# A pair's scale factors taken apart from its rotation, and accumulating DMAs issued some products later, in a two-layer encoder on one Trainium2 core

## The chip, the core and the metric

The kernel runs on one core of a Trainium2 chip. A core has five engines, each with a queue of its own that it works through in order: TensorE (PE, products of a stationary and a moving operand into PSUM banks), VectorE (DVE), ScalarE (ACT), GpSimd (POOL) and SyncE (SP, which here only issues loads). DMAs are issued by an engine's queue (here SP, ACT and POOL) and moved by 16 DMA engines beside it. Engines wait for one another by semaphores: an instruction whose input isn't ready holds up everything behind it on its own engine, and nothing else.

The metric is the device time of one execution in microseconds, the median over several.

## The reference

The reference is an encoder of two layers over 512 tokens of width 1024, all in float32. Layer 0 mixes tokens by gated linear attention, layer 1 by softmax attention, and a gated MLP with a width-3 convolution follows each. The change lies wholly in layer 1's attention:

```python
def attn_mixer(h, w_qkv, q_norm, k_norm, w_out, cos, sin):
    proj = h @ w_qkv
    q, k, v = jnp.split(proj, [...])          # 8 query heads, 2 key/value heads of 128
    q = apply_rope(rmsnorm(q, q_norm), cos, sin)
    k = apply_rope(rmsnorm(k, k_norm), cos, sin)
    ...
    s = jnp.einsum('bkgqd,bksd->bkgqs', q_blk, k) * scale   # four query heads share a kv head
    p = jax.nn.softmax(s, axis=-1)
    ... jnp.einsum('bkgqs,bksd->bkgqd', p, v) ...
    return o @ w_out

def apply_rope(x, cos, sin):
    half = x.shape[-1] // 2
    x1, x2 = x[..., :half], x[..., half:]
    return jnp.concatenate([x1 * cos - x2 * sin, x1 * sin + x2 * cos], axis=-1)
```

The root mean square in `rmsnorm` is one number per token and head, so it commutes with the rotation: a head may be rotated first and scaled afterwards.

## The kernel before, in words

**Split products.** The large products take their operands in the type float32r. Every operand is kept as two parts, `hi` (the value as it is written into that type) and `lo` (the rest), and a product is three matmuls: hi·hi, hi·lo and lo·hi (`mm3`). A product of 128 rows by 512 columns over one chunk of 128 is called a step below; a projection of one tile has 8 chunks (`KC`), that is 8 steps or 24 matmuls.

**Weights.** `Weights` takes weight blocks in a written order. `half(src, n)` gives out the half block that is asked for, and makes one more ahead of need: SP loads a raw block of 1 MB (two buffers `raw`), ACT writes `wh`, and `lo` arises in one of two ways. In `split` DVE subtracts. For the sources in `by_dma` (all the weights of layer 1's attention: `qk_order`, `w_av`, `w_aout`) ACT writes the negated `hi` into `wl`, and POOL issues a DMA that adds `raw` into `wl` (line 125). There are three buffers of `wh` and three of `wl`.

**Attention.** Heads are made in pairs: `kpair` makes the two key heads, `qpair(i)` the query heads 2i and 2i+1, and both go through the generator `roped`, which yields at the end of each small piece of work, so that the caller can weave pieces of several generators into one another. In `roped`, 16 pieces are the steps of the two halves A and B of the pair (their banks of tag `acc`, three in all). Then ACT squares A and B and DVE adds the squares (`qa`). Then come four pieces with one product each of A or B with the norm's weight and a table of cosines or sines (`rt`, DVE, line 627). Then `scale_tok` makes the factors per token and head: PE sums the squares over the partitions (`hs`, line 603), DVE scales and adds epsilon (`hs`, line 607; `hr`, line 186), POOL raises to the power -1/2 (`hr`, line 190), and DVE multiplies the result into `qsc` (line 610). Then four subtractions and additions of 64 rows make the rotated heads (`ry`, lines 636 and 637; on POOL but for the key pair's and query pair 0's subtractions), and at last ACT and DVE split each head into `hi` and `lo` (`q`, lines 643 and 644).

The scores run over 32 blocks, 8 heads by 4 groups of 128 queries, one after the other, with block t as a beat: `scores` (PE `s`, then DVE's maximum `mx` and factor `nb`, then ACT's exponential `p` with the row sum), then the pieces of other generators that `plan[t]` holds, then `turn` of the block four beats earlier (PE transposes `pt`, ACT `pth`, DVE `ptl`), then `shares` (DVE `rc` and the normalised `p`), then every second beat `mix` of a block six beats earlier (PE `po`, and per head a split `oT`). Two banks serve `s`, two `pt`, one `po`. `Q_STEPS` and `Q_READY` say at which beats how many pieces of the query pairs 1 to 3 run: the 16 steps from the first, the rest from the second. Head 2i's first scores stand at beat 8i and need its `hi` and `lo`. `O_STEPS` are the beats at which a step of the output projection (`op`, `out_steps`, line 297) runs; its remaining steps follow after the last beat.

**What sets the order.** The program's order is a wish: the framework's scheduler puts each engine's instructions into a fixed order when the kernel is built, by priority and by when it thinks that inputs are ready, and that order can be read before the kernel runs.

Of the kernel before, what the change touches and what calls it, by code (L numbers as in the profile page):

```python
# [8 lines left out]
F32 = mybir.dt.float32  # L9
# [37 lines left out]
def hybrid_encoder_kernel(  # L47
# [55 lines left out]
    class Weights:  # L103
# [1 line left out]


        def __init__(self):
            self.todo, self.made, self.raw, self.by_dma = [], {}, {}, []

        def add(self, src):  # L110
            for i in range(src.shape[0]):
# [2 lines left out]
        def make(self, key):  # L114
            src, i, h = key
            if h == 0 and (id(src), i) not in self.raw:
                t = sp.tile([P, 4 * S], F32, tag="raw", bufs=2, name=nm("raw"))
                sync.dma_start(t, src[i])
                self.raw[id(src), i] = t
            r = self.raw[id(src), i][:, h * 2 * S : (h + 1) * 2 * S]  # L120
            hi, lo = pair("wh", 3, F32R, "wh"), pair("wl", 3, F32R, "wl")
            if any(src is a for a in self.by_dma):
                act.activation(hi, r, AF.Copy)
                act.activation(lo, r, AF.Copy, scale=-1.0)  # L124
                pool.dma_start(lo.bitcast(F32), r, accum_op=ALU.add)  # L125
# [56 lines left out]
    def rsqrt_eps(src, w, n, scale=None, tag="tiny"):  # L182

        t = tiny(w, n, tag)
        if scale is None:
            dve.tensor_scalar(t, src, EPS, None, ALU.add)
        else:
            dve.tensor_scalar(t, src, scale, EPS, ALU.mult, ALU.add)
        r = tiny(w, n, tag)
        pool.tensor_tensor(r, t, halfneg[:, :w], ALU.pow)  # L190
        return r
# [52 lines left out]
    def mm3(ps, wh, wl, mh, ml, start, stop):  # L244

        mm(ps, wh, mh, start=start, stop=False)  # L246
        mm(ps, wh, ml, start=False, stop=False)  # L247
        mm(ps, wl, mh, start=False, stop=stop)  # L248
# [12 lines left out]
    def token_steps(src, i0, hl, ps, width, per_half):  # L261

        for hf in range(KC // per_half):
            wh, wl = W.half(src, i0 + hf)
            for kk in range(per_half):
                k = hf * per_half + kk
                sl = slice(kk * width, (kk + 1) * width)
                for j in range(NT):
                    js = slice(j * P, (j + 1) * P)
                    xh, xl = hl[k][0][:, js], hl[k][1][:, js]  # L270
                    st, sp_ = k == 0, k == KC - 1
                    mm(ps[j][:, :width], xh, wh[:, sl], start=st, stop=False)
# [8 lines left out]
    def out_steps(src, hl, nxt):  # L281


        pss, ws = {}, {}

        def part(ng, ks):
            if ng not in pss:
                pss[ng] = [bank("s" if ng % 2 else "acc", "op") for _ in range(2)]
            for k in ks:
                hf, kk = divmod(k, 4)  # L290
                if (ng, hf) not in ws:
                    ws[ng, hf] = W.half(src, ng * 2 + hf)
                wh, wl = ws[ng, hf]
                for i, (wt, mv) in enumerate(((wh, hl[k][0]), (wh, hl[k][1]), (wl, hl[k][0]))):
                    for n in range(2):
                        sl = slice((kk * 2 + n) * P, (kk * 2 + n + 1) * P)
                        mm(pss[ng][n], wt[:, sl], mv, start=k == 0 and i == 0, stop=k == KC - 1 and i == 2)  # L297
                yield

        def end(ng):  # L300
            for n in range(2):
                c = ng * 2 + n
                dve.tensor_tensor(x[c], x[c], pss[ng][n], ALU.add)
                nxt.chunk(c)

        yield from part(0, range(6))
        yield from part(1, range(6))
        for ng in range(2):
            yield from part(ng, (6, 7))
            end(ng)  # L310
        for ng in (2, 3):
            yield from part(ng, range(KC))
            end(ng)
# [278 lines left out]
    def attention(norm, nxt):  # L592
# [3 lines left out]
        cos, sin = cs[:, :S], cs[:, S:]  # L596
        r2 = cp.tile([P, NT], F32, name="r2")

        def scale_tok(sq, extra, keep):

            ps = bank("pt", "hs")
            for j in range(NT):
                mm(ps[:, 2 * j : 2 * j + 2], sq[:, j * P : (j + 1) * P], bd, start=True, stop=True)
            t = tiny(8, "hs", "tiny2")
            t3 = t.rearrange("p (j e) -> p j e", e=2)
            bc = lambda a: a.rearrange("p (j o) -> p j o", o=1).to_broadcast([P, NT, 2])
            dve.tensor_tensor(t3, ps[:, :8].rearrange("p (j e) -> p j e", e=2), bc(r2), ALU.mult)
            r = rsqrt_eps(t, 8, "hr", tag="tiny2")
            o = cp.tile([P, 8], F32, name=nm(keep))
            dve.scalar_tensor_tensor(o.rearrange("p (j e) -> p j e", e=2), r.rearrange("p (j e) -> p j e", e=2),  # L610
                                     extra, bc(norm.rtok), ALU.mult, ALU.mult)
            return o

        def roped(i, wcol, extra, keep, tag="acc"):
# [8 lines left out]
            yield  # L623
            wa, wb = prm[:, wcol : wcol + 1], prm[:, wcol + 1 : wcol + 2]
            t = [tmp("u", "rt") for _ in range(4)]
            for dst, src, w, tab in ((t[0], pa, wa, cos), (t[2], pa, wa, sin), (t[1], pb, wb, sin), (t[3], pb, wb, cos)):
                dve.scalar_tensor_tensor(dst, src, w, tab, ALU.mult, ALU.mult)
# [65 lines left out]
        run(qg, 5)  # L693
        run(vg2, 3)
        whole(qg)
        whole(vg2)
# [172 lines left out]
```

## Time and profile before

| | us |
|---|---|
| three runs | 1147.37, 1147.58, 1147.93 (median 1147.58) |
| profiled execution, its own time | 1146.72 |
| its span, from the first to the last instruction | 1145.0 |
| PE busy in the span | 1131.7 (99%) |
| DVE, ACT, POOL busy | 683.7, 485.0, 87.5 |
| granted TensorE clock | 1.000 |

The attention of layer 1 takes the span from about 590 to 780 us. The profile's rows give a start and a duration in us (the waits views: total, times, longest), the engine, the line of the source, the operation and its tiles as out<-in. "[x <-E tile L]" behind a row of the timeline is the idle time of its engine before it and what ended it. Matmuls overlap in the pipeline, so a matmul's own duration is longer than the distance of its start to the next start, and the distance is what it costs.

### The profile page before, as it was taken

How to read it: one execution, taken by the hardware profiler on the slowest of the kernel's cores; microseconds unless marked ns; L12 is line 12 of the kernel's file. 1: busy time of each engine (PE TensorE's matmuls, PEld its weight loads, DVE VectorE, ACT ScalarE, POOL GpSimd, SP SyncE). 2: the span in 40 equal slices, each digit the busy share in tenths (PEclk: the TensorE clock that was granted, in tenths of full speed). 3: DMA queues.
4: the chain of work that ended last, by engine and by line, in shares of the span. 5: the costliest groups of instructions: out<-in, count | busy, mean ns of one | idle time of the engine just before them, and what ended most of it. 6: DMA issues, size and time to landing. Idle time of an engine off the chain costs nothing. (4 is left out here: it accounts for less than half of the span.)

```text
span 1145.0 us, 13049 instructions
## 1 busy us (share of the span) xinstructions
PE 1131.7 (99%) x5280; PEld 942.3 (82%) x5280; DVE 683.7 (60%) x992; ACT 485.0 (42%) x695; POOL 87.5 (8%) x77
## 2 busy tenths in 40 slices
PE   9999999999999999999999999999999999999998
PEld 7888888888888888888888877888888888888887
DVE  5677653577777777633326678745777777762221
ACT  5565233444444444422244656554444444441210
POOL 0214110000000000000004423010000000000000
PEclk9999999999999999999999999999999999999999
DMA  6322211232322323323256532253322322323320
GB/s 228 135 86 74 76 72 37 74 103 81 110 82 102 111 76 108 110 74 111 98 147 160 148 74 74 56 111 111 110 98 86 110 80 104 110 76 127 129 92 19
DMA packets 20412, 113.76 MB, mean 99 GB/s; under 512 B 2432, under 2 KB 2816, under 8 KB 8832
## 3 DMA queue, kind: packets, MB, share of 16 engines
q1 hardware_dynamic: 17328, 102.42, 25.8%
q0 software_dynamic: 2880, 10.49, 4.8%
q8 instruction: 41, 0.67, 0.3%
q14 instruction: 19, 0.16, 0.0%
q10 hardware_dynamic: 144, 0.02, 0.0%
HBM read 100.34 MB, written 2.10 MB: 89 GB/s over the span
## 5 line engine op out<-in xcount | busy, mean ns | idle before, releaser
L134 ACT ACTIVATE wh<-raw 128x1024 fp32r<-128x1024 f32 x160 | 168.8, 1056 | 335.6 <-PE up L247 132.4
L135 DVE TENSOR_TENSOR wl<-raw,wh 128x1024 fp32r<-128x1024 f32 x160 | 198.9, 1244 | 150.2 <-ACT wh L134 149.8
L246 PE MATMUL up<-xhl,wh 128*128 128x512 f32 x704 | 274.3, 390 | 0.0
L248 PE MATMUL up<-xhl,wl 128*128 128x512 f32 x704 | 273.9, 389 | 0.0
L247 PE MATMUL up<-xhl,wh 128*128 128x512 f32 x704 | 273.9, 389 | 0.0
L248 PEld LDWEIGHTS up<-xhl,wl 128*128 128x128 f32 x704 | 132.1, 188 | 27.5
L246 PEld LDWEIGHTS up<-xhl,wh 128*128 128x128 f32 x704 | 132.1, 188 | 27.4
L247 PEld LDWEIGHTS up<-xhl,wh 128*128 128x128 f32 x704 | 132.2, 188 | 27.3
L248 PE MATMUL dn<-gu,wl 128*128 128x512 f32 x352 | 136.9, 389 | 0.0
L246 PE MATMUL dn<-gu,wh 128*128 128x512 f32 x352 | 136.9, 389 | 0.0
L247 PE MATMUL dn<-gu,wh 128*128 128x512 f32 x352 | 136.9, 389 | 0.0
L564 DVE TENSOR_TENSOR u<-up,R 128x512 f32<-128x512 f32 x88 | 60.3, 687 | 52.7 <-PE up L248 52.6
L566 ACT ACTIVATE y<-u,cw 128x512 f32<-128x512 f32 x88 | 71.1, 810 | 21.6 <-DVE u L564 21.6
L248 PEld LDWEIGHTS dn<-gu,wl 128*128 128x128 f32 x352 | 66.1, 188 | 13.8
L247 PEld LDWEIGHTS dn<-gu,wh 128*128 128x128 f32 x352 | 66.1, 188 | 13.7
L246 PEld LDWEIGHTS dn<-gu,wh 128*128 128x128 f32 x352 | 66.1, 188 | 13.7
L297 PE MATMUL op<-oT,wh 128*128 128x512 f32 x256 | 70.6, 394 | 0.0
L568 DVE SCALAR_TENSOR_TENSOR y<-u,cw,y 128x511 f32<-128x511 f32 x88 | 65.9, 751 | 2.9
L567 DVE SCALAR_TENSOR_TENSOR y<-u,cw,y 128x511 f32<-128x511 f32 x88 | 65.5, 745 | 0.6 <-ACT y L566 0.6
L570 ACT ACTIVATE y<-y 128x512 f32<-128x512 f32 x44 | 27.9, 634 | 87.8 <-DVE y L568 87.7
L297 PEld LDWEIGHTS op<-oT,wh 128*128 128x128 f32 x256 | 47.1, 188 | 9.6 <-ACT oT L524 0.3
L125 POOL DMA_DIRECT2D wl<-raw x20 | 17.8, 888 | 461.9 <-ACT wl L124 461.9
(190 smaller groups left out, 1553.3 us busy)
## 6 DMA issues: line engine op xcount, KB each, us to landing
raw<-in_w_up_dram SPq DMA_DIRECT2D x44, 1024.0 KB, 4.8
raw<-in_w_down_dram SPq DMA_DIRECT2D x22, 1024.0 KB, 4.8
wl<-raw POOLq DMA_DIRECT2D x20, 512.0 KB, 4.6
raw<-in_w_vg_dram SPq DMA_DIRECT2D x6, 1024.0 KB, 4.8
raw<-in_w_akq_dram SPq DMA_DIRECT2D x5, 1024.0 KB, 5.1
raw<-in_w_kq_dram SPq DMA_DIRECT2D x4, 1024.0 KB, 4.8
raw<-in_w_gout_dram SPq DMA_DIRECT2D x4, 1024.0 KB, 4.8
raw<-in_w_aout_dram SPq DMA_DIRECT2D x4, 1024.0 KB, 4.8
```

The lines of the kernel that those rows point to most:

```text
L125: pool.dma_start(lo.bitcast(F32), r, accum_op=ALU.add)
L134: act.activation(hi[:, sl], r[:, sl], AF.Copy)
L135: dve.tensor_tensor(lo[:, sl], r[:, sl], hi[:, sl].bitcast(F32), ALU.subtract)
L246: mm(ps, wh, mh, start=start, stop=False)
L247: mm(ps, wh, ml, start=False, stop=False)
L248: mm(ps, wl, mh, start=False, stop=stop)
L297: mm(pss[ng][n], wt[:, sl], mv, start=k == 0 and i == 0, stop=k == KC - 1 and i == 2)
L564: dve.tensor_tensor(u, ps, norm.R, ALU.mult)
L566: act.activation(y, u, AF.Identity, scale=w(1), bias=w(3))
L567: dve.scalar_tensor_tensor(y[:, 1:], u[:, : S - 1], w(0), y[:, 1:], ALU.mult, ALU.add)
L568: dve.scalar_tensor_tensor(y[:, : S - 1], u[:, 1:], w(2), y[:, : S - 1], ALU.mult, ALU.add)
L570: act.activation(res[1], res[1], AF.Silu)
```

## The change

Five edits, all in what builds the attention:

1. `scale_tok` is cut in two. Its first part (PE `hs`, DVE `hs` and `hr`, POOL `hr`) is a piece of its own after the first of the four `rt` products, and `scale_end` (DVE `qsc`) a piece of its own after the third. A pair has one piece more.
2. `Q_STEPS` and `Q_READY` are written anew: query pair 1's steps end one beat earlier and its other pieces start one beat earlier, as do pair 2's; the other pieces of pair 3 start at beat 20 as before, with four in each of the first two beats. `O_STEPS` has 23 in the place of 24.
3. The accumulating DMA of line 125 isn't issued in `make` any more. It goes on a list, and `flush` issues it some steps into the next products, or at the next `half`.
4. `by_dma` holds a count: the second half of the output projection's weights (`w_aout` blocks 2 and 3, four halves) is split by ACT and DVE, without a negated copy and without a DMA.
5. The pieces ahead of the beats (`run(...)`) are dealt out in other portions.

```diff
-Q_STEPS = {1: (0, (4, 3, 3, 3, 3)), 2: (5, (3, 2, 2, 2, 2, 2, 3)), 3: (12, (2,) * 8)}
-Q_READY = {1: (5, (4, 3, 2, 1)), 2: (12, (3, 3, 2, 1, 1)), 3: (20, (3, 3, 2, 1, 1))}
-O_STEPS = (22, 24, 25, 27, 29, 31, 32, 33, 34, 35, 36, 37)
+Q_STEPS = {1: (0, (4,) * 4), 2: (4, (3, 3, 2, 2, 2, 2, 2)), 3: (11, (2, 2, 2, 2, 2, 2, 2, 1, 1))}
+Q_READY = {1: (4, (3, 3, 3, 1, 1)), 2: (11, (3, 3, 2, 1, 1, 1)), 3: (20, (4, 4, 1, 1, 1))}
+O_STEPS = (22, 23, 25, 27, 29, 31, 32, 33, 34, 35, 36, 37)
...
-            if any(src is a for a in self.by_dma):
+            if any(src is a and i < n for a, n in self.by_dma):
                 act.activation(hi, r, AF.Copy)
                 act.activation(lo, r, AF.Copy, scale=-1.0)
-                pool.dma_start(lo.bitcast(F32), r, accum_op=ALU.add)
+                self.pending.append((lo, r))
...
+        def flush(self):
+            for lo, r in self.pending:
+                pool.dma_start(lo.bitcast(F32), r, accum_op=ALU.add)
+            self.pending = []
...
     def half(self, src, n):
         key = (id(src), n // 2, n % 2)
+        self.flush()
...
-    W.by_dma += qk_order + [w_av, w_aout]
+    W.by_dma += [(a, 1) for a in qk_order + [w_av]] + [(w_aout, 2)]
...
             mm3(ps, wh[:, sl], wl[:, sl], *hl[k], k == 0, k == KC - 1)
+            if k == 2:
+                W.flush()
             yield
...
                     mm(ps[j][:, :width], xl, wh[:, sl], start=False, stop=sp_)
+                if kk == 1:
+                    W.flush()
                 yield
...
                         mm(pss[ng][n], wt[:, sl], mv, start=k == 0 and i == 0, stop=k == KC - 1 and i == 2)
+                W.flush()
                 yield
...
-        def scale_tok(sq, extra, keep):
+        def scale_tok(sq):
             ps = bank("pt", "hs")
             ...
-            dve.tensor_tensor(t3, ps[:, :8]..., bc(r2), ALU.mult)
-            r = rsqrt_eps(t, 8, "hr", tag="tiny2")
+            dve.tensor_tensor(by_two(t), by_two(ps[:, :8]), by_block(r2), ALU.mult)
+            return rsqrt_eps(t, 8, "hr", tag="tiny2")
+
+        def scale_end(r, extra, keep):
             o = cp.tile([P, 8], F32, name=nm(keep))
-            dve.scalar_tensor_tensor(o..., r..., extra, bc(norm.rtok), ALU.mult, ALU.mult)
+            dve.scalar_tensor_tensor(by_two(o), by_two(r), extra, by_block(norm.rtok), ALU.mult, ALU.mult)
             return o
...
-            for dst, src, w, tab in ((t[0], pa, wa, cos), (t[2], pa, wa, sin), (t[1], pb, wb, sin), (t[3], pb, wb, cos)):
-                dve.scalar_tensor_tensor(dst, src, w, tab, ALU.mult, ALU.mult)
-                yield
-            sc = scale_tok(qa, extra, keep)
+            turned(0)
+            yield
+            r = scale_tok(qa)
+            yield
+            turned(1)
+            yield
+            turned(2)
+            yield
+            sc = scale_end(r, extra, keep)
+            yield
+            turned(3)
             yield
...
         run(qg, 4)
-        run(kg, 5)
+        run(kg, 2)
         run(qg, 2)
-        run(kg, 3)
+        run(kg, 7)
         run(qg, 8)
         kk = whole(kg)
         run(qg, 2)
...
-        run(qg, 5)
+        run(qg, 2)
+        run(vg2, 1)
+        run(qg, 6)
         run(vg2, 3)
         whole(qg)
```

(`turned(n)` is the n-th product of the old loop.)

Built, the two kernels have the same order on every engine through the first layer, its MLP and the attention's projections up to about 638 us of the profile before (2735 of PE's rows, 526 of DVE's, 374 of ACT's, 55 of POOL's are the same in kind and order). So edits 3 and 5 move nothing in that part, and the orders differ only from the beats onwards. There POOL has 78 rows for 82, ACT 646 for 650 and DVE 998 for 994.

More of the change, by code (lines that the diff above doesn't have):

```diff
@@ L107, in __init__ @@
         def __init__(self):
-            self.todo, self.made, self.raw, self.by_dma = [], {}, {}, []
+            self.todo, self.made, self.raw, self.by_dma, self.pending = [], {}, {}, [], []
         def add(self, src):
@@ L597, in attention @@
         r2 = cp.tile([P, NT], F32, name="r2")
-        def scale_tok(sq, extra, keep):
+        by_block = lambda a: a.rearrange("p (j o) -> p j o", o=1).to_broadcast([P, NT, 2])
+        by_two = lambda a: a.rearrange("p (j e) -> p j e", e=2)
+        def scale_tok(sq):
             ps = bank("pt", "hs")
@@ L604, in scale_tok @@
             t = tiny(8, "hs", "tiny2")
-            t3 = t.rearrange("p (j e) -> p j e", e=2)
-            bc = lambda a: a.rearrange("p (j o) -> p j o", o=1).to_broadcast([P, NT, 2])
-            dve.tensor_tensor(t3, ps[:, :8].rearrange("p (j e) -> p j e", e=2), bc(r2), ALU.mult)
-            r = rsqrt_eps(t, 8, "hr", tag="tiny2")
+            dve.tensor_tensor(by_two(t), by_two(ps[:, :8]), by_block(r2), ALU.mult)
+            return rsqrt_eps(t, 8, "hr", tag="tiny2")
+        def scale_end(r, extra, keep):
             o = cp.tile([P, 8], F32, name=nm(keep))
-            dve.scalar_tensor_tensor(o.rearrange("p (j e) -> p j e", e=2), r.rearrange("p (j e) -> p j e", e=2),
-                                     extra, bc(norm.rtok), ALU.mult, ALU.mult)
+            dve.scalar_tensor_tensor(by_two(o), by_two(r), extra, by_block(norm.rtok), ALU.mult, ALU.mult)
             return o
@@ L625, in roped, with turned @@
             t = [tmp("u", "rt") for _ in range(4)]
-            for dst, src, w, tab in ((t[0], pa, wa, cos), (t[2], pa, wa, sin), (t[1], pb, wb, sin), (t[3], pb, wb, cos)):
+            rt = ((t[0], pa, wa, cos), (t[2], pa, wa, sin), (t[1], pb, wb, sin), (t[3], pb, wb, cos))
+            def turned(n):
+                dst, src, w, tab = rt[n]
                 dve.scalar_tensor_tensor(dst, src, w, tab, ALU.mult, ALU.mult)
-                yield
-            sc = scale_tok(qa, extra, keep)
+            turned(0)
[9 more added lines that the diff above has]
+            turned(3)
             yield
```

## The prediction

> **What bounds the kernel now.** I read the page's busy shares first, then who waited for whom on PE, then the same for DVE and POOL, and last the timelines around PE's waits.
>
> ```profile
> span 1145.0 us, 13049 instructions
> ...
> PE 1131.7 (99%) x5280; PEld 942.3 (82%) x5280; DVE 683.7 (60%) x992; ACT 485.0 (42%) x695; POOL 87.5 (8%) x77
> ```
>
> PE is busy in 1131.7 of 1145.0 us. No product is added or taken away by the change, so it can win only PE's idle time and what PE's order of instructions costs. Only the beats of the second layer's attention and the output projection behind them are ordered anew, so that idle time alone counts which lies there:
>
> ```profile
> PE s L248 <- DVE q L644: 2.7, 1, 2.7
> PE pt L737 <- DVE ptl L741: 1.4, 1, 1.4
> PE op L297 <- DMA wl<-raw: 1.0, 1, 1.0
> PE s L246 <- ACT p L719: 0.8, 1, 0.8
> ```
>
> These four waits (total, times, longest) are 2.7 + 1.4 + 1.0 + 0.8 = 5.9 us. What stands behind them shows in the waits of POOL and DVE from 630 to 782 us:
>
> ```profile
> POOL wl L125 <- ACT wl L124: 96.2, 12, 21.3
> ...
> DVE qsc L610 <- POOL hr L190: 8.6, 4, 3.1
> ```
>
> DVE stood 8.6 us at the factor `qsc` of four pairs, up to 3.1 us at a time, because POOL's power was late. For query pair 1, on POOL, DVE and PE in turn:
>
> ```profile
> 655.14 1.28 POOL L637 TENSOR_TENSOR ry<-rt,rt 64x512 f32<-64x512 f32 x1
> 656.50 1.66 POOL L190 TENSOR_TENSOR hr<-hr,halfneg 128x8 f32<-128x8 f32 x1
> ```
>
> ```profile
> 658.20 0.17 DVE L610 SCALAR_TENSOR_TENSOR qsc<-hr,rtok 128x8 f32<-128x8 f32 x1 [3.08 <-POOL hr L190]
> 658.28 0.68 DVE L741 TENSOR_TENSOR ptl<-pt,pth 128x512 fp32r<-128x512 f32 x1
> 658.88 0.15 DVE L724 RECIPROCAL rc<-sm 128x1 f32<-128x1 f32 x1
> 658.95 0.67 DVE L716 TENSOR_REDUCE mx<-s 128x1 f32<-128x512 f32 x1
> 659.54 0.48 DVE L725 TENSOR_SCALAR p<-p,rc 128x512 f32<-128x512 f32 x1
> 659.93 0.21 DVE L717 TENSOR_SCALAR nb<-mx,qsc 128x1 f32<-128x1 f32 x1
> 660.06 0.68 DVE L644 TENSOR_TENSOR q<-ry,q 128x512 fp32r<-128x512 f32 x1
> ```
>
> ```profile
> 660.79 0.50 PE L248 MATMUL s<-k,q 128*128 128x512 f32 x1 [2.68 <-DVE q L644]
> ```
>
> POOL finished the pair's four `ry`, 1.36 us from start to start, before it came to the power (656.50, 1.66 us). DVE, in order, stood 3.08 us until 658.20, then first did the block that had queued up, and the split `q` at 660.06 came so late that PE waited 2.68 us with the third product of head 2's first scores. For pair 3 it is the same:
>
> ```profile
> 710.74 1.67 POOL L190 TENSOR_TENSOR hr<-hr,halfneg 128x8 f32<-128x8 f32 x1
> ```
>
> ```profile
> 712.44 0.17 DVE L610 SCALAR_TENSOR_TENSOR qsc<-hr,rtok 128x8 f32<-128x8 f32 x1 [2.45 <-POOL hr L190]
> ```
>
> The stop of 2.45 us at 712.44 is what PE's waits for `ptl` (1.4) and `p` (0.8) come from: both stand behind it in DVE's queue. The sources of 4.9 of the 5.9 us are thus POOL's order and DVE's early place of `qsc`.
>
> **Pair 1.** In the changed order POOL has the power ahead of the four `ry`, and DVE has a `ptl`, a normalised `p` and a maximum between `hr` and `qsc`. By the rows above these take 0.60 + 0.39 + 0.59 and `rc` 0.07, 1.65 us in all, and the power takes 1.66: DVE arrives at `qsc` about when it is ready. What is late next is the rotated head, as `ry` now ends after the power. These rows price the chain and PE's walk:
>
> ```profile
> L719 ACT ACTIVATE p<-s,nb,qsc 128x512 f32<-128x512 f32 x32 | 24.8, 776 | 19.9 <-DVE nb L717 19.7
> ...
> L627 DVE SCALAR_TENSOR_TENSOR rt<-B,prm,rope 128x512 f32<-128x512 f32 x6 | 4.4, 740 | 0.0
> ...
> L643 ACT ACTIVATE q<-ry 128x512 fp32r<-128x512 f32 x6 | 3.7, 628 | 1.3 <-POOL ry L637 1.3
> ```
>
> ```profile
> 690.29 0.60 PE L737 MATMUL pt<-ident,p 128*128 128x128 f32 x4
> 690.65 0.47 PE L246 MATMUL s<-k,q 128*128 128x512 f32 x1
> ...
> 691.43 0.39 PE L246 MATMUL B<-xhl,wh 128*128 128x512 f32 x1
> ...
> 692.79 0.60 PE L737 MATMUL pt<-ident,p 128*128 128x128 f32 x4
> 693.15 0.36 PE L246 MATMUL po<-pth,vh 128*128 128x256 f32 x1
> ...
> 694.65 0.40 PE L246 MATMUL s<-k,q 128*128 128x512 f32 x1
> ```
>
> From start to start four transposes cost 0.36, a score's three products behind them 0.78, six products of a step 1.36, twelve of `po` 1.50. Between `hs` and the third product of head 2's first scores the changed order has 2 products, `pt`, `s`, 9 products, `pt`, `s`, 6, `pt`, `s`, 6, `pt`, `po` and two of `s`: 0.45 + 0.36 + 0.78 + 2.04 + 0.36 + 0.78 + 1.36 + 0.36 + 0.78 + 1.36 + 0.36 + 1.50 + 0.55 = 11.0 us (in the old order 6, `pt`, `s`, 6, `pt`, `po` and two of `s`: 6.3). Against that, POOL's chain: about 1.0 for DVE's small steps and one `rt` (0.74), power 1.66, two `ry` 2.7, ACT's copy 0.63, DVE's `lo` 0.68, and 0.3 for handing over (an estimate): 7.0. And DVE's own queue: the maximum of the last block ahead of `q` can start 7.3 us into the walk, and with `mx`, `ptl`, `p`, `nb` and `q` (0.59 + 0.60 + 0.39 + 0.13 + 0.68) and 0.2 it is done at 9.9. Both come before 11.0, so the 2.7 us go. What is added: `hs` now stands 2.4 us behind the pair's last product (three scores and seven products). ACT there copies a weight (1.06) ahead of squaring B (0.59), and DVE adds (0.68): 2.3 to 2.5. I put a new wait of 0.2 us on PE, between 0 and 0.8.
>
> **Pair 2** has a walk of 13.3 us by the same prices against the same chain of 7.0, and PE waited nothing for it before. Cost 0.
>
> **Pair 3.** From `hs` to the third product of head 6's first scores the changed order has `pt`, two of `s`, two of `po`, `pt`, eight of `po`, `s`, six of `op`, `pt`, `s`, six of `op`, `pt`, `po` and two of `s`: 9.4 us by the same prices (one step of `op` was moved here by the 23 in `O_STEPS`). POOL here makes both subtractions first, so head 6 needs three `ry`: 1.0 + 1.66 + 4.1 + 0.63 + 0.68 + 0.3 = 8.4. That fits, with 1.0 to spare. But ACT's order has both heads' copies ahead of an exponential: the second copy ends at 1.0 + 1.66 + 5.4 + 0.1 + 0.63 = 8.8, the exponential (0.78) at 9.6, and the bank that it frees is wanted by PE at 8.9. I put 0.8 us of waits on PE here, 0.6 at this bank and 0.2 at the next, between 0 and 2.2 (as much as now).
>
> **Deferred DMAs.** `flush` moves each accumulating DMA in POOL's queue past nothing but POOL's own rows; PE doesn't hold it. In the built order two of them stand just ahead of the powers of pairs 1 and 3, and each waits for ACT's negated copy. Counted from the last product of pair 3's B, ACT is through with that copy at about 4.0 us and POOL with the DMA (0.88) at 4.9, when DVE's `hr` is ready, also at 4.9. Cost 0; what it costs if the cover is gone is the slower rival.
>
> **Output projection.** Four of its halves lose the DMA. The last wait of PE and its cause, with ACT's copy of the same half and DVE's price for a subtraction:
>
> ```profile
> 769.91 0.73 PE L297 MATMUL op<-oT,wl 128*128 128x512 f32 x2 [1.00 <-DMA wl<-raw]
> ```
>
> ```profile
> 759.31 1.05 ACT L123 ACTIVATE wh<-raw 128x1024 fp32r<-128x1024 f32 x1
> ```
>
> ```profile
> L135 DVE TENSOR_TENSOR wl<-raw,wh 128x1024 fp32r<-128x1024 f32 x160 | 198.9, 1244 | 150.2 <-ACT wh L134 149.8
> ```
>
> PE got a DMA's `lo` at 769.91, 1.00 us late. ACT's `wh` ends at 760.4; with a subtraction of 1.24 behind it, and 2 us for whatever DVE has first, `lo` is there at 763.7, five us early. The wait of 1.0 goes, and four subtractions (5.0 us of DVE) lie beside PE's products. The first of them stands ahead of the last `ptl`:
>
> ```profile
> 746.76 0.69 DVE L741 TENSOR_TENSOR ptl<-pt,pth 128x512 fp32r<-128x512 f32 x1 [1.18 <-ACT pth L740]
> ```
>
> ```profile
> 750.07 0.28 PE L246 MATMUL po<-pth,vh 128*128 128x256 f32 x1
> ```
>
> That `ptl` ended at 747.45 and was used at 750.07: 2.6 us of room for 1.24. Cost 0.
>
> **Split transposes.** In the old order eight groups of four transposes are cut by a block's scores or by `op`, in the new one a single group:
>
> ```profile
> 723.42 0.27 PE L737 MATMUL pt<-ident,p 128*128 128x128 f32 x1
> 723.63 0.50 PE L246 MATMUL s<-k,q 128*128 128x512 f32 x1
> ...
> 724.43 0.49 PE L737 MATMUL pt<-ident,p 128*128 128x128 f32 x3
> 724.68 0.36 PE L246 MATMUL po<-pth,vh 128*128 128x256 f32 x1
> 724.88 0.28 PE L247 MATMUL po<-ptl,vh 128*128 128x256 f32 x1
> ```
>
> One transpose, three score products, three transposes: 1.26 us, and the first product after takes 0.20 from start to start where 0.12 is the rate of `po` (1.50 by 12), so 1.34. Uncut it is 0.36 + 0.78 = 1.14. Seven cuts fewer are 7 x 0.20 = 1.4 us, between 0 and 1.6.
>
> **The sum.** Against the profiled execution's own 1146.72 us: -2.7 + 0.2 (pair 1), -2.2 + 0.8 (pair 3), -1.0 (DMA), -1.4 (cuts): -6.3, so 1140.4. The runs' median stands 0.86 above that execution: 1141.3 us.
>
> **Rivals.** *DVE held by POOL.* The wait at `qsc` comes back as slower DVE instructions (min, median, max ns of one):
>
> ```profile
> L725 DVE TENSOR_SCALAR p<-p,rc x32: 475/478/1570, 638.1 to 739.1; 128x512 f32<-128x512 f32 x32
> ```
>
> The normalised `p` takes 0.48 us on the median, but once 1.57: that one ran at 652.4, among pair 1's `ry`, and was held 1.1 us. If in pairs 1 and 3 it is held for 0.6 by the power and twice for 1.1 by `ry`, DVE is 2.8 us late; of that 1.1 and 1.0 are spare, so PE waits 1.7 + 1.8 more: 1141.3 + 3.5 = 1144.8. [...] The row of 1.57 agrees; that the median is 0.48 says that it seldom strikes, and I give it 0.18.
>
> *The heads are late instead.* If ACT's second copy or POOL's `ry` fall behind PE's walk, the waits for `q` return in full and only the DMA's 1.0 and the cuts' 1.4 are won: 1147.58 - 2.4 = 1145.2. For it speaks that the power now delays all `ry`; against it the 11.0 and 9.4 us of walk. 0.08.
>
> *Slower: a deferred DMA holds POOL.* POOL stood 96.2 us in 12 times before such DMAs, 8.0 on the mean, and now two powers, and with them `ry` and `q`, stand behind one. If each is held for 8.0 and 1.1 and 1.0 are spare, PE loses 6.9 + 7.0: 1141.3 + 13.9 = 1155.2. It turns into a loss once the two holds exceed 4.2 us each (1.05 and half of 1147.6 - 1141.3 = 6.3). It would take a raw block that arrives late; the copies' inputs were loaded long before. 0.06.
>
> **How the numbers follow.** My forecast has 0.64; 0.04 is left for what I haven't seen, spread around no change. A measurement of this kernel can tell about 0.2% (2.3 us) from no change. Faster than 1145.3: the forecast, the first rival, and half of the second, which sits at that limit: 0.86. Slower than 1149.9: 0.06 and a little, 0.07. Between: 0.07. The low end takes all waits and eight cuts away: 1147.58 - 5.9 - 1.6 = 1140.1, and 0.3 for the spread of runs, 1139.8. The high end takes in the unknown bounds and the first rival and reaches the second: 1145.2.
>
> **What would show it.** Right: PE's list of waits without `op` on a DMA, with `s` on `q` under 1 us, DVE's wait at `qsc` down from 8.6 to about 2 (8.6 less 3.08, 2.45 and some 1.2 for pairs 1 to 3; pair 0 keeps its own), PE idle from 638 us to the end of the projection near 1 us, and transposes in fours. Wrong: `p` rows above 1 us in number with PE waits on `ptl` or `q` (first rival); a long idle on POOL before `wl` with `hr` right behind it (slower); or a new wait of PE on a DMA.

## The result, and the profile after

The changed kernel takes 1140.30 us (median; 1140.29 to 1140.32), the kernel before, run beside it, 1147.55 (1147.37 to 1147.93): a ratio of 0.9936, 95% interval 0.9919 to 0.9954. Forecast were 1141.3 us and a range of 1139.8 to 1145.2.

The page of the changed kernel, its span and the busy shares:

```profile
span 1138.6 us, 13034 instructions
...
PE 1130.0 (99%) x5280; PEld 942.2 (83%) x5280; DVE 688.5 (60%) x996; ACT 481.7 (42%) x691; POOL 84.3 (7%) x73
```

PE has the same 5280 products and is busy 1.7 us less; the span is 6.4 us shorter. Whom PE waited for from 590 to 800 us (total, times, longest), and then the two lines on POOL and DVE from 630 to 782:

```profile
PE s L253 <- ACT p L748: 0.8, 1, 0.8
PE s L255 <- DVE q L671: 0.3, 1, 0.3
```

```profile
POOL wl L133 <- ACT wl L124: 59.4, 8, 13.3
...
DVE qsc L625 <- POOL hr L197: 1.9, 1, 1.9
```

The profile before has one wait more than the four of the forecast, for pair 3's `hs`:

```profile
PE hs L603 <- DVE nb L717: 0.2, 1, 0.2
```

Of these five waits with 6.0 us, two with 1.1 are left. DVE's 8.6 us at the factor are down to 1.9, all of it pair 0's own. How POOL and DVE now meet in query pair 1, first POOL, then DVE:

```profile
649.76 1.71 POOL L197 TENSOR_TENSOR hr<-hr,halfneg 128x8 f32<-128x8 f32 x1 [0.82 <-DVE rc L753]
651.40 1.27 POOL L663 TENSOR_TENSOR ry<-rt,rt 64x512 f32<-64x512 f32 x1
```

```profile
649.45 0.16 DVE L193 TENSOR_SCALAR hr<-hs 128x8 f32<-128x8 f32 x1
649.52 0.16 DVE L753 RECIPROCAL rc<-sm 128x1 f32<-128x1 f32 x1
650.34 0.69 DVE L770 TENSOR_TENSOR ptl<-pt,pth 128x512 fp32r<-128x512 f32 x1 [0.67 <-ACT pth L769]
650.95 0.48 DVE L754 TENSOR_SCALAR p<-p,rc 128x512 f32<-128x512 f32 x1
651.34 0.69 DVE L745 TENSOR_REDUCE mx<-s 128x1 f32<-128x512 f32 x1
651.94 0.76 DVE L625 SCALAR_TENSOR_TENSOR qsc<-hr,rtok 128x8 f32<-128x8 f32 x1
```

The power runs at 649.76 with a whole block's DVE work beside it. DVE comes to `qsc` at 651.94 and doesn't stand in front of it, but the little instruction itself takes 0.76 us, where it took 0.17 before: it runs beside POOL's first `ry`. And pair 3, ACT first, then PE:

```profile
709.35 0.63 ACT L670 ACTIVATE q<-ry 128x512 fp32r<-128x512 f32 x1 [0.80 <-POOL ry L664]
709.88 0.76 ACT L748 ACTIVATE p<-s,nb,qsc 128x512 f32<-128x512 f32 x1
```

```profile
710.79 0.50 PE L253 MATMUL s<-k,q 128*128 128x512 f32 x1 [0.79 <-ACT p L748]
```

That is the new wait of the forecast: ACT has the second head's copy ahead of the exponential whose bank PE wants, and PE loses 0.79 us.

For the runs below one more number is used, the **stage**: from the start of the first score product to the start of the first product of the MLP behind the output projection (`up`), read from the timeline of PE. It leaves out the start of the kernel: the first score comes between 630.5 and 633.8 us in the profiles. Taken off it are PE's listed waits; what is left is "the rest".

| kernel | median us | ratio to before, 95% | stage | PE's waits in it | rest |
|---|---|---|---|---|---|
| before | 1147.5 | | 148.82 | 5.99 | 142.83 |
| changed | 1140.30 | 0.9936 [0.9919, 0.9954] | 142.85 | 1.07 | 141.78 |
| e1, DMAs at once | 1140.60 | 0.9934 [0.9922, 0.9946] | 142.94 | 1.10 | 141.84 |
| e2, factor ended at once | 1144.20 | 0.9966 [0.9954, 0.9978] | 146.61 | 3.66 | 142.95 |
| e3, old factor, new beats | 1145.33 | 0.9979 [0.9970, 0.9988] | 148.47 | 4.41 | 144.06 |
| e4, 24 for 23 | 1140.95 | 0.9937 [0.9926, 0.9949] | 143.56 | 0.82 | 142.74 |
| e5, before + split by DVE | 1146.52 | 0.9992 [0.9983, 1.0001] | 148.94 | 4.97 | 143.97 |
| e6, before + factor | 1142.88 | 0.9961 [0.9948, 0.9975] | 143.86 | 1.85 | 142.01 |
| e7, before + beats | 1146.12 | 0.9989 [0.9980, 0.9998] | 148.75 | 4.39 | 144.36 |
| e8, pair 2's head early | 1140.48 | 0.9944 [0.9932, 0.9956] | 142.69 | 1.15 | 141.54 |
| e9, pair 3's copy late | 1140.77 | 0.9944 [0.9931, 0.9956] | 143.01 | 0.61 | 142.40 |
| e10, copy between | 1139.58 | 0.9931 [0.9918, 0.9945] | 141.94 | 0.49 | 141.45 |
| e11, factor on POOL | 1140.44 | 0.9939 [0.9927, 0.9952] | 142.46 | 0.99 | 141.47 |

In e6 pair 0's `hs` stands ahead of the first score, so that its stage and its rest lack some 0.8 us of products that the others have in them. The stages of e3, e5 and e7 hold a fall of PE's clock (under e3).

From before to changed the stage is 5.97 us shorter: 4.92 of it are waits, 1.05 the rest.

### The profile page after: what moved, and what is told of

It reads as the page before. It is cut to its first block, busy times and chain, and to the rows that moved or that the text cites. A ratio compares the mean times of both kernels' runs of the same rounds, so it can differ in the third digit from the quotient of the medians.

```text
span 1138.6 us, 13034 instructions
## 1 busy us (share of the span) xinstructions
PE 1130.0 (99%) x5280; PEld 942.2 (83%) x5280; DVE 688.5 (60%) x996; ACT 481.7 (42%) x691; POOL 84.3 (7%) x73
## 5 line engine op out<-in xcount | busy, mean ns | idle before, releaser
L140 ACT ACTIVATE wh<-raw 128x1024 fp32r<-128x1024 f32 x164 | 173.0, 1056 | 337.9 <-PE up L254 132.0
L141 DVE TENSOR_TENSOR wl<-raw,wh 128x1024 fp32r<-128x1024 f32 x164 | 204.0, 1244 | 149.5 <-ACT wh L140 149.1
L281 PE MATMUL vg<-wh,xhl 128*128 128x512 f32 x128 | 50.1, 396 | 0.2 <-ACT wh L140 0.2
```

What stands on the lines that cost most here:

```text
L140: act.activation(hi[:, sl], r[:, sl], AF.Copy)
L141: dve.tensor_tensor(lo[:, sl], r[:, sl], hi[:, sl].bitcast(F32), ALU.subtract)
```

## The experiments

**The parts, one by one.** Four of the runs take one part alone, or leave one out.

e6, the kernel before with `scale_tok` cut in two and nothing else (the piece more goes into each pair's second beat, and for the pairs made ahead of the beats into two of the `run` portions):

```diff
-            for dst, src, w, tab in (...):
-                dve.scalar_tensor_tensor(dst, src, w, tab, ...); yield
-            sc = scale_tok(qa, extra, keep)
+            turned(0); yield
+            r = scale_tok(qa); yield
+            turned(1); yield
+            turned(2); yield
+            sc = scale_end(r, extra, keep); yield
+            turned(3)
...
+Q_READY = {1: (5, (4, 4, 2, 1)), 2: (12, (3, 4, 2, 1, 1)), 3: (20, (3, 4, 2, 1, 1))}
```

> The kernel before with one edit: the factor begun behind the first rt and ended in a piece of its own, with the one piece more added to the second of each pair's beats. In the built order POOL has the power ahead of all ry in pairs 2 and 3 and between them in pair 1, and the eight cuts of transposes remain. Theory as it stands after the first four runs (what costs PE is DVE held at qsc, by the power and then by POOL's next ry, and behind it rt, ry, q and an exponential): pair 3's waits (2.2 us) go, pair 1's shrink by about half: 1143.8 us (1142.5 to 1145.0). Rival (the walk of the new beats is needed for the heads to be in time): 1146 or more.

Measured: 1142.88, that is 4.6 below before. PE's waits:

```profile
PE hs L606 <- DVE nb L730: 0.7, 1, 0.7
PE pt L750 <- DVE ptl L754: 0.5, 1, 0.5
PE op L297 <- DMA wl<-raw: 0.4, 1, 0.4
PE s L246 <- ACT p L732: 0.3, 1, 0.3
```

The 2.7 for `q` is gone with the old beats too, where the expectation had left about half of it. From the first product behind pair 1's `hs` to the third product of head 2's first scores PE walks 7.2 us here (652.71 to 659.90) and 11.1 in the changed kernel, so the longer walk isn't what it takes. The factor's two pieces carry most of the gain.

e7, the kernel before with the new beats alone:

```diff
+Q_STEPS = {1: (0, (4,) * 4), 2: (4, (3, 3, 2, 2, 2, 2, 2)), 3: (11, (2, 2, 2, 2, 2, 2, 2, 1, 1))}
+Q_READY = {1: (4, (3, 3, 2, 1, 1)), 2: (11, (3, 3, 1, 1, 1, 1)), 3: (20, (4, 3, 1, 1, 1))}
+O_STEPS = (22, 23, 25, ...)
```

> The kernel before with one edit: the new beats (Q_STEPS, Q_READY with the old number of pieces, O_STEPS). POOL has the power behind the ry in all three pairs; cuts fall from eight to one. Theory: as the changed kernel with the old factors, with the DMA's wait of 1.0 us on top: 1146.4 us (1145.4 to 1147.2). Rival (beats bring most of the gain on their own): 1143 or less.

Measured: 1146.12 (ten runs from 1144.60 to 1147.10; an eleventh took 2951.96, and the median with it is 1146.28). The time is close to the one expected, but it is made up of other terms: the waits fell only from 5.99 to 4.39, and the rest rose by 1.5, although the cut transposes are gone here. What raised it stands under e3. The DMA's wait of 1.0, which the expectation had on top, isn't among PE's listed waits here, though the DMAs are all kept.

e3, the changed kernel with the factors made behind all four `rt` and in one piece, as before; the pieces' count is kept:

```diff
-            turned(0); yield
-            r = scale_tok(qa); yield
-            turned(1); yield
-            turned(2); yield
-            sc = scale_end(r, extra, keep); yield
-            turned(3); yield
+            for n in (0, 1, 2, 3):
+                turned(n); yield
+            r = scale_tok(qa)
+            sc = scale_end(r, extra, keep); yield
+            yield
```

> The changed kernel, but the factors are made as before, behind all four products of the rotation and in one piece; beats, DMAs and the number of pieces stay as changed. POOL has the power behind the rotation's subtractions and additions again. Theory (the power behind ry is what held DVE and PE): DVE stands at qsc for about 3 us again; the longer walk of PE takes up most of it in pair 1 (0.3 to 0.5 us lost), and pair 3 loses 1.5: 1142.3 us (1141.3 to 1143.5). Rival (the beats alone bring the gain): 1140.3 to 1140.6.

Measured: 1145.33 (1144.44 to 1148.35), 5.0 above the changed kernel and 3.0 above what was expected. PE's waits, and DVE's at the factor:

```profile
PE s L253 <- ACT p L743: 2.0, 1, 2.0
PE s L253 <- ACT q L665: 1.6, 2, 1.2
PE s L255 <- DVE q L666: 0.6, 2, 0.3
PE pt L761 <- DVE ptl L765: 0.3, 1, 0.3
```

```profile
DVE qsc L625 <- POOL hr L197: 8.5, 4, 3.1
```

DVE stands 8.5 us again. The waits are 3.3 us more than in the changed kernel, not the 2 that I had expected, and the rest is 2.3 more. The longest, 1.98 us in pair 3, comes by way of ACT: the exponential that frees the bank stood 3.04 us for the block's `nb`, which is behind `qsc` in DVE's queue:

```profile
713.84 0.78 ACT L743 ACTIVATE p<-s,nb,qsc 128x512 f32<-128x512 f32 x1 [3.04 <-DVE nb L741]
```

Part of the rest is PE's clock. The same place in e7's profile, PE's products behind its wait of 1.98 us, and the granted clock (the number behind PE's busy time) in steps of half a microsecond:

```profile
715.16 0.50 PE L246 MATMUL s<-k,q 128*128 128x512 f32 x1 [1.98 <-ACT p L719]
715.50 0.40 PE L247 MATMUL s<-k,q 128*128 128x512 f32 x1
715.74 0.39 PE L248 MATMUL s<-k,q 128*128 128x512 f32 x1
...
718.33 0.63 PE L246 MATMUL s<-k,q 128*128 128x512 f32 x1
718.76 0.63 PE L247 MATMUL s<-k,q 128*128 128x512 f32 x1
719.19 0.63 PE L248 MATMUL s<-k,q 128*128 128x512 f32 x1
```

```profile
716.00:716.50 0.50, 0.50 (x6) 1.00 0.00 0
716.50:717.00 0.50, 0.50 (x3) 0.62 0.00 0
717.00:717.50 0.50, 0.50 (x3) 0.50 0.00 0
...
719.50:720.00 0.50, 0.50 (x2) 0.50 0.00 0
720.00:720.50 0.50, 0.50 (x6) 0.96 0.00 0
```

Behind the wait the clock falls to half for 3.4 us, and score products start 0.43 us apart instead of 0.23: half of 3.4, 1.7 us, are lost on top of the wait (an estimate from the clock of 0.50). e3's profile has the same fall behind its own wait of 1.98 (0.50 in the windows from 715.5 to 718.5), and e5's at the wait of 2.68 (0.50 from 662.5 to 665.5). (In e3 the other 0.6 of the rest are four waits more than in the changed kernel, each of which costs 0.16 beyond what is listed, as is worked out below.) So behind waits of 1.98 and 2.68 us another 1.7 us can be lost. It does not happen each time: the profile of before has the same wait of 2.68 at the full clock (1.00 in the windows from 656 to 666), and e3's runs fall into two groups, 1144.44 to 1144.92 and 1145.73 to 1146.15, with one at 1148.35. Behind e2's wait of 1.70, below, the clock stayed at 1.00 (710 to 718).

e5, the kernel before with the second half of the output projection's weights split by DVE:

```diff
-            if any(src is a for a in self.by_dma):
+            if any(src is a and i < n for a, n in self.by_dma):
...
+    W.by_dma += [(a, 1) for a in qk_order + [w_av]] + [(w_aout, 2)]
```

> The kernel before with one edit: the second half of the output projection's weights is split by ACT and DVE instead of by accumulating DMAs. Every other queue keeps its order. Theory (the DMA's late lo cost PE 1.0 us, and DVE's four subtractions are covered): 1146.4 us, that is 1.0 to 1.2 below the kernel before, and PE has no wait for a DMA. Rival (the next transfer or DVE is late in its place): within 0.3 of the kernel before.

Measured: 1146.52 (1145.19 to 1148.53), 0.95 less than before. PE's wait for the DMA is gone, those for `q`, `ptl` and `p` are the old 2.7, 1.4 and 0.8. (The interval touches 1; the term is shown by the wait that went, more than by the time.)

The three parts alone make 4.6 + 1.4 + 0.95 = 6.9 us, all together 7.2. That is nearly a sum, but not one of separate terms: the DMA's wait of 1.0 went in e5 and left PE's list in e7 too, and PE's waits fell by 4.1, 1.6 and 1.0 us one by one, but by 4.9 together.

e1, the changed kernel with the accumulating DMA issued at once:

```diff
-                self.pending.append((lo, r))
+                pool.dma_start(lo.bitcast(F32), r, accum_op=ALU.add)
```

> The changed kernel with the accumulating DMAs issued at once, behind ACT's negated copy, instead of some products later. Theory (POOL's order is all that a later issue can change, and here it changes nothing, as no instruction of POOL stands between the two places): 1140.3 us, within 0.1. Rival (the deferral frees POOL, so that part of the gain is its own): above 1140.8.

Measured: 1140.60 (1140.24 to 1141.05), and the built order is the same on every engine. Deferring them does nothing here; the 0.3 lies in this kernel's spread of 0.8.

**Why the factor needs a piece of its own.** e2 ends it at once, behind its first part; built, only DVE's order differs:

```diff
             r = scale_tok(qa)
+            sc = scale_end(r, extra, keep)
             yield
             turned(1)
             yield
             turned(2)
             yield
-            sc = scale_end(r, extra, keep)
             yield
             turned(3)
```

> The changed kernel, but the factor is begun ahead and ended at once: DVE has qsc straight behind hr, so that it waits for POOL's power (1.66 us) in each of the pairs 1 to 3. POOL's and PE's orders are as in the changed kernel. Theory (DVE's late work has about 1.1 us of room before PE waits): DVE is about 1.6 us later, PE waits 0.5 more in pair 1 and 0.5 more in pair 3: 1141.3 us (1140.6 to 1142.3). Rival (only POOL's order matters, DVE had idle time enough): 1140.3, within 0.2.

Measured: 1144.20, 3.9 above the changed kernel, where 1.0 was expected. Pair 3 on DVE, ACT and PE:

```profile
706.69 1.26 DVE L625 SCALAR_TENSOR_TENSOR qsc<-hr,rtok 128x8 f32<-128x8 f32 x1 [0.94 <-POOL hr L197]
...
708.54 1.02 DVE L754 TENSOR_SCALAR p<-p,rc 128x512 f32<-128x512 f32 x1
709.48 0.20 DVE L746 TENSOR_SCALAR nb<-mx,qsc 128x1 f32<-128x1 f32 x1
```

```profile
709.77 0.78 ACT L748 ACTIVATE p<-s,nb,qsc 128x512 f32<-128x512 f32 x1 [2.65 <-DVE nb L746]
```

```profile
710.70 0.50 PE L253 MATMUL s<-k,q 128*128 128x512 f32 x1 [1.70 <-ACT p L748]
```

I had counted only DVE's stop and its spare time. But the stop of 0.94 is followed by two holds beside POOL's `ry` (1.26 us for the small product, 1.02 for the normalised `p` that takes 0.48 alone), and the block's `nb` stands behind all three: it starts 5.5 us behind DVE's `hs` (709.48 against 703.94), and in the changed kernel 3.0 (703.92 against 700.97), where it is ahead of `qsc`. ACT's exponential stands 2.65 us for `nb`, and PE 1.70 for the bank that the exponential frees. The path goes DVE, ACT, PE; my price stopped at DVE. Of the 3.66 us of waits in e2, 2.50 are for exponentials that waited for `nb` in this way:

```profile
PE s L253 <- ACT p L748: 2.5, 3, 1.7
```

The last `rt` is late as well, and POOL's additions and ACT's second copy with it, but in pair 3 PE has no wait of its own for these.

**The terms that were left.** e4 puts the output projection's step back to beat 24. Then seven groups of four transposes are cut instead of one (seven in the profile, not the eight that the expectation names):

```diff
-O_STEPS = (22, 23, 25, ...)
+O_STEPS = (22, 24, 25, ...)
```

> The changed kernel with the second step of the output projection at beat 24 again instead of 23. The built order then has eight cut groups of transposes instead of one, and pair 3's walk is one step (1.4 us) shorter. Theory (a cut costs 0.20 us of PE): 1.4 us more for seven cuts, and up to 1 us for the shorter walk: 1142.3 us (1141.6 to 1143.0). Rival (a cut costs nothing, what counts is the walk): 1140.3 to 1141.3, all of it as waits of PE for q.

Measured: 1140.95. The waits are 0.25 less and the rest is 0.96 more: 0.16 us for each of six cuts, less than the 0.20 taken. The time is below the range that the theory gave, by the smaller price and because the shorter walk cost nothing; it lies in the rival's, but what the rival said, all of it as waits for `q`, didn't come.

e9 has pair 3's last piece one beat later, so that the second copy stands behind the exponential; more groups of transposes are cut with it (eight in the built order, not the seven that the expectation names, so seven more than in the changed kernel):

```diff
-... 3: (20, (4, 4, 1, 1, 1))}
+... 3: (20, (4, 4, 1, 1, 0, 1))}
```

> Edit: the changed kernel with pair 3's last piece (the second head's copy and split) one beat later, so that on ACT it stands behind the exponential whose bank PE waited 0.79 us for. Built, seven groups of four transposes are cut by scores or by the output projection, instead of one. Theory (a late copy and cut transposes each have a price of their own): the wait of 0.8 goes, six cuts more cost 0.16 each as where O_STEPS had 24 again, 1.0: 1140.3 - 0.8 + 1.0 = 1140.5, with the stage's time outside PE's listed waits at 141.78 + 1.0 = 142.8. Rival (cut transposes cost nothing; what O_STEPS with 24 lost came from the step of the output projection that it moved): 1140.3 - 0.8 = 1139.5, with 141.8 outside the waits.

Measured: 1140.77. The waits fall by 0.46 (to 0.3 for the exponential's bank and 0.3 for pair 2's `q`), the rest grows by 0.62, 0.09 for each of seven cuts. The theory holds in kind: cuts cost something, but 0.09 to 0.16 and not 0.20, and the wait did not go wholly.

e8 has pair 2's split of the head earlier:

```diff
-... 2: (11, (3, 3, 2, 1, 1, 1)), ...
+... 2: (11, (3, 3, 3, 1, 0, 1)), ...
```

> The changed kernel with pair 2's pieces dealt as (3, 3, 3, 1, 0, 1) instead of (3, 3, 2, 1, 1, 1): in the built order head 4's lo stands one block of scores earlier in DVE's queue, and ACT has head 4's copy ahead of a weight copy. Nothing else is changed on PE or POOL. Theory (the wait of 0.3 us of PE for q in pair 2 is DVE's queue): that wait goes, 1139.9 us. Rival (it only moves to the next instruction): 1140.3.

Measured: 1140.48. The 0.3 for `q` is gone and stands at another place, so the rival was right:

```profile
PE po L254 <- DVE ptl L770: 0.3, 1, 0.3
```

e11 takes the factor's last product to POOL:

```diff
-            dve.scalar_tensor_tensor(by_two(o), by_two(r), extra, by_block(norm.rtok), ALU.mult, ALU.mult)
+            f = norm.rtok if extra == 1.0 else rx        # rx = rtok * HD ** -0.5, once, by DVE
+            pool.tensor_tensor(by_two(o), by_two(r), by_block(f), ALU.mult)
```

> Edit: the changed kernel with the factor's last product made by POOL (a product of the power with the token factor, times 128 to the power -1/2, which DVE makes once per layer) instead of DVE's scalar_tensor_tensor, so that DVE no longer stands at it beside POOL's subtraction. Theory (the stops of 0.76, 1.26 and 1.14 us that DVE had at the factor beside POOL's rotation lie beside other work and cost PE nothing; POOL's chain to pair 3's copies does cost): DVE's waits at the factor vanish, POOL has one more small instruction ahead of the second ry, some 0.3 us, and PE's wait of 0.8 for the exponential grows by that: 1140.6, between 1140.3 and 1141.3. Rival (DVE held by POOL is what makes the remaining waits of 0.8 and 0.3): both go, 1139.2.

Measured: 1140.44. On POOL the product takes 0.2 us; DVE's normalised `p`, on the other hand, is now held in all three pairs (1.02, 1.00 and 1.01 us; in pair 3, shown here, 1.01); PE's list has one wait:

```profile
705.00 0.19 POOL L627 TENSOR_TENSOR qsc<-hr,r 128x8 f32<-128x8 f32 x1
```

```profile
705.83 1.01 DVE L757 TENSOR_SCALAR p<-p,rc 128x512 f32<-128x512 f32 x1
```

```profile
PE s L253 <- ACT p L751: 1.0, 1, 1.0
```

The wait of 0.8 is there without any hold of DVE at `qsc`, and 0.2 longer; POOL's new instruction of 0.2 ahead of the later `ry` fits that. The holds at `qsc` thus cost little in the changed kernel (at most the 0.3 for pair 2's `q`, which went with them). What all of DVE's holds cost isn't shown: with those of `p` there are still 1.6 us of them here, and 3.5 in the changed kernel.

e10 has pair 2's last piece one beat later. In the built order pair 3's first `ry` then stands ahead of its power, and its second copy behind the exponential, with no more cuts:

```diff
-... 2: (11, (3, 3, 2, 1, 1, 1)), ...
+... 2: (11, (3, 3, 2, 1, 1, 0, 1)), ...
```

> Edit: the changed kernel with pair 2's last piece one beat later, which also lets the built order place pair 3's first rotated quarter differently; on ACT pair 3's second copy now stands behind the exponential and one transposed block, and the groups of transposes stay whole but for one. Theory (the 0.8 us wait comes from ACT's order alone): that wait goes, DVE's 0.3 for pair 2's head may stay or grow as its split stands later, up to 0.6: 1140.3 - 0.8 + 0.2 = 1139.7. Rival (POOL's chain, not ACT's order, is what is late): the wait comes back at the head itself, as s on q of pair 3, and the time stays at 1140.3 or rises by up to 0.5.

Measured: 1139.58 (1139.28 to 1139.77), the best of all kernels here, 0.7 below the changed one (from runs of another session; the ranges don't meet). ACT in pair 3, and PE's waits:

```profile
707.99 0.63 ACT L670 ACTIVATE q<-ry 128x512 fp32r<-128x512 f32 x1 [1.13 <-POOL ry L664]
708.53 0.76 ACT L748 ACTIVATE p<-s,nb,qsc 128x512 f32<-128x512 f32 x1
...
709.28 0.59 ACT L769 ACTIVATE pth<-pt 128x512 fp32r<-128x512 f32 x1
709.76 0.63 ACT L670 ACTIVATE q<-ry 128x512 fp32r<-128x512 f32 x1
```

```profile
PE s L255 <- DVE q L671: 0.3, 1, 0.3
PE s L253 <- ACT p L748: 0.2, 1, 0.2
```

The exponential runs at 708.53 instead of 709.88 and the second copy at 709.76, without a wait of its own. The bank's 0.8 is down to 0.2, and the time is near the theory's 1139.7. The run doesn't separate ACT's order from POOL's, though: with one `ry` (at 702.11) ahead of the power (at 703.57) POOL's chain is another too.

## Why the prediction was right, point by point

**Right in mechanism and nearly in size.** Of the terms of the sum, the waits were to change by -2.7 + 0.2 - 2.2 + 0.8 - 1.0 = -4.9 us; the profile has -4.92. That the two agree to 0.02 is luck: three terms of 0.2 to 0.3 that were wrong or missing (pair 1's 0.2, pair 2's 0.28, and the 0.21 at pair 3's `hs`, which stood in the profile before and went) make each other up.

- *Pair 1.* The 2.7 for `q` went. The walk was 11.1 us, as said (11.0), but DVE's queue took 10.8 of it and not 9.9 (from 648.53 to 659.29, for a product at 659.65): 0.4 us to spare, not 1.1. And e6 lost the 2.7 with a walk of 7.2, so it was the place of the power and of `qsc` that did it. Of the 0.2 put at `hs` nothing shows.
- *Pair 2.* Put at 0; 0.28 us came, for the third score product on DVE's `q`. e8 shows that this is not that one split's place: moved earlier, it leaves the same 0.3 at a `ptl`.
- *Pair 3.* The 1.4 for `ptl` went, and the wait for the exponential was forecast with its place and its size: 0.79 us at the bank behind ACT's second copy, against 0.6 there and 0.2 at the next.
- *DMA.* The 1.0 went, and e5 prices it alone at 0.95. But it left PE's list with the beats alone too (e7), so how much of it is the split's in the changed kernel stays open.
- *Deferral and the first subtraction ahead of `ptl`.* 0 as said (e1, and no wait of PE there). The slower rival needed POOL held by a DMA; POOL's waits at them fell from 96.2 us to 59.4 (8 times for 12, as four DMAs are gone), and in pairs 1 and 3 POOL stands idle for 0.82 and 0.33 us between the DMA and the power.

**Mis-sized: the cuts.** I took 7 x 0.20 = 1.4 us. The rest of the stage fell by 1.05, and not all of that is cuts: a product is recorded 0.39 us long, but the next one starts 0.23 behind it, so that a stop of PE shows 0.16 less than it costs. Three waits fewer (two for five) are 0.5 of the 1.05. That leaves some 0.6 for seven cuts, 0.08 each; e9 has 0.09 and e4 0.16. So the same 0.16 was missing from each wait, 0.5 in all, and the cuts were priced 0.8 too high; that the one made up for much of the other is luck.

**Mis-sized: the step from the profiled execution to the median.** I carried 0.86 us over from before to after. It did not come: the changed kernel's runs stand on its profile, 1140.29. Without it the sum had said 1140.4. The likely cause is the clock behind long waits, but no profile of the kernel before shows it; what is on record fits it. In the later sessions the kernel before ran 47 times; the 13 executions with a mean granted clock of 1.000 took 1145.75 to 1146.75 us, median 1146.16, the 34 with 0.999 or less 1146.76 to 1150.05. The profiled one was of the first kind, the median of the second. e5 has the same wait of 2.68: two of its runs, at 1.000, took 1145.19 and 1145.22, eight at 0.999 took 1146.40 to 1146.85, and the one at 1148.53 is the profile with the fall behind that wait. (A mean of 0.999 alone doesn't prove it: e10's profile has it too, with 1.00 in all its windows from 631 to 773 us.) Read so, the 7.25 us between the medians are about 5.9 of the stage (1146.16 - 1140.30; the stage itself says 5.97) and some 1.4 that the old waits cost in clock. Against the profiled executions the sum said 6.3 us; they differ by 6.4, with some 0.5 of it ahead of the stage, where both kernels have the same order.

**The first rival** (DVE held by POOL) has its holds shown and not its price. I had called it seldom because the normalised `p` takes 0.48 us on the median of 32. That was the wrong count: few of the 32 run beside a `ry` at all. In the profile before three do, and two of these took 1.57 and 1.07 (652.37 and 705.73 us); DVE's `hr`, which I didn't look at, took 0.95 and 1.16 us in pairs 1 and 3 where it takes 0.16 alone. The rows give the shortest, median and longest in ns, for `hr` in the profile before and for `p` in the changed kernel:

```profile
L186 DVE TENSOR_SCALAR hr<-hs x5: 161/950/1164, 612.1 to 708.2; 128x8 f32<-128x8 f32 x5
```

```profile
L754 DVE TENSOR_SCALAR p<-p,rc x32: 475/480/1143, 637.6 to 732.8; 128x512 f32<-128x512 f32 x32
```

In the changed kernel it struck `qsc` in all three pairs (0.76, 1.26 and 1.14 us for 0.17) and two `p` (0.65 and 1.14), 3.5 us in all; the 0.6 a time that the rival had from the power is shown by no run: beside the power `p` kept its 0.48 (at 650.95 and 674.93). That this costs PE so little is a matter of what stands behind the held instruction. In pair 3 the block's `nb` is ahead of `qsc`; e2 puts it behind, and PE waits 1.70 us with the scores that need the exponential's bank, where the changed kernel waits nothing. e11 takes the holds at `qsc` away, and the time is the same; a kernel without any hold was not run. **The second rival** (heads late) fell with the 0.3 for `q`. Of what was to be seen, PE's idle time near 1 us (1.07), DVE's wait at `qsc` near 2 (1.9), no `op` on a DMA and transposes in fours (31 groups of 32 in the built order) all came.

**Where the expectations failed** was in e2 and e3, and in e4 by the price of a cut. In e2 and e3 the change, taken back in part, loses more than I priced: I had set DVE's stop against DVE's own spare time, and not followed what stands behind it. That is `nb`, for which ACT's exponential waits, for whose bank PE waits.

## What to carry to other kernels

When a small step on a slow engine (here POOL's power, 1.66 us for 128 x 8) is awaited in order by a busy one, start it early and put the waiting instruction a block's work behind it; then see what that instruction has behind it that feeds another engine, because a stop travels on through that and not through the waiter's own work. In a kernel like this one, price a wait of the matrix engine at what the list shows and the 0.16 us that it hid here, and allow for the clock: behind waits of 1.98 and 2.68 us another 1.7 us was lost in some executions, which the one profiled need not show. Count how often one engine holds another only among the instructions that run beside it, not among all of a form. And when parts of a change are tried alone, compare the waits and not only the times: here the times nearly added up (6.9 for 7.2 us), though the parts share a term.

## What the runs showed of the hardware

**The clock behind a wait.** Not expected: waits of 1.98 us (e7 and e3) and 2.68 us (e5) were followed by 3.4 us at half the clock (0.50 in the windows). The fall began 0.2 us before the products ran again in e5, 0.7 us after that in e3 and 1.5 us after it in e7; these times, and the 3.4 us, are estimates from the share of half the clock in the first and the last window of half a microsecond. The same wait of 2.68 us in the profile of before, and e2's of 1.70, had 1.00 throughout. What decides which executions are hit is not shown by any run here.

**DVE held by POOL.** In the changed kernel the product of 128 x 8 on DVE (`qsc`) took 0.17 us without a `ry` beside it (pair 0, at 635.54) and 0.76 to 1.26 when it began inside one of POOL's `ry` of 64 x 512, and it ended with it: in pair 1 at 651.94 + 0.76 = 652.70, POOL's `ry` at 651.40 + 1.27 = 652.67. Four of the changed kernel's 32 `p` run beside a `ry`. The two that began well inside one took 0.65 and 1.14 us:

```profile
707.02 1.14 DVE L754 TENSOR_SCALAR p<-p,rc 128x512 f32<-128x512 f32 x1
```

The two that began at the edge of one kept 0.48 and 0.49, and behind the latter (653.96) the `ry` took 1.47 us instead of 1.28. Instructions that read a PSUM bank kept their time beside `ry` (`rt` 0.74 at 705.11, `ptl` 0.68 at 705.77, `mx` 0.67 at 679.01), and so did those of 128 x 1 (`nb` 0.20 at 680.17). What is named here as held, `qsc`, `p`, `hr` and in pair 0 of the changed kernel a split `q` (1.55 us for 0.68, at 625.88), reads no PSUM bank. No run was made to test whether that is what sets them apart.
